# Sums of weight quarters in program order, and x_c tiles split three behind their load, in a two-layer hybrid trunk in fp32

## The chip, the cores and the metric

One core of one Trainium2 chip. The metric is the device time of the whole kernel in microseconds (us); lower is better. Three runs of the kernel before took 1402.33, 1403.09 and 1404.14 us; the median is 1403.09 us.

## What is computed

A trunk of two layers over 256 context and 256 latent tokens of width 1024, one batch element. Layer 0 mixes tokens with a bidirectional mLSTM, layer 1 with multi-head latent attention; a gated feed-forward with a convolution follows each, and every sub-layer has an adaptive shift and scale and a LayerNorm behind it. Cut to the part around the change, the inputs of the mLSTM (T is the tokens, M_INNER is 2048):

```python
def _mlstm_inputs(h, w_up, conv_w, conv_b, w_qk, w_v, w_gates, b_gates):
    x_m = h @ w_up                                        # [T, 2048]
    x_c = jax.nn.silu(_dwconv(x_m, conv_w, conv_b))       # convolution over tokens
    q, k = jnp.split(x_c @ w_qk, 2, axis=-1)
    ...
    v = (x_m @ w_v).reshape(B, T, M_HEADS, M_DV).transpose(0, 2, 1, 3)
    gates = jnp.einsum("bti,zig->zbgt", x_c, w_gates) + b_gates[:, None, :, None]
```

All of it is fp32. The kernel reaches that accuracy with three matmuls in a rounded format for each product: every operand is split into a high half (a cast) and a low half (the operand minus the cast), and high x high, high x low and low x high are added up.

## The kernel before

TensorE does one product after another: w_up, the output gate ("og"), x_m times w_v (w_v, L771 to L833), the gates (from L841), q and k, the scan, and so on. `mm3` (L373 to L377) issues the three matmuls of a product, at L375, L376 and L377.

**The stream of weights.** Weights come in "quarters" of 128 x 1024 numbers, in one fixed list. Class `Stream` (L229) takes each through three steps. `_load` (L262) issues its DMA from DRAM, from SyncE's queue (L273), into a "raw" buffer; in w_v there are several rings of such buffers. `_split` (L288) makes the halves: ScalarE casts the raw quarter to the high half (L315), then VectorE subtracts to get the low half (L318), both into one of three "w" buffers (NB = 3). `use` (L324) hands the halves to TensorE; when a quarter is done, its w buffer is free for the quarter three places on.

**The product w_v.** It is a Strassen-Winograd product: fewer matmuls, with sums of blocks of the weights in place of some blocks, and sums of partial products at the end. It has two passes, p = 0 and p = 1. Each has a first loop of 16 quarters (vt2, v11, vt3 and vt1, four times) and a second of 12 (v21, vt4 and v22, four times), and each quarter has 12 matmuls of 128 x 512. Counted along the list, pass p = 1 has the quarters 60 to 75 and 76 to 87. Of each four quarters of a first loop, three hold sums of weights that are made on the spot by `_sum` (L278): VectorE adds v12 and v22 in place (L284, the quarter vt3), adds v11 to that (L285, the quarter vt2, which has no load of its own), and adds v11 to v12 (L286, the quarter vt1). `_split` calls `_sum` four quarters ahead of the vt1 quarter (SUMS = 5 counts the quarter itself). vt2 is also written to DRAM (L317), and read back and added to v22's weights for vt4 (L270, L271).

**The tiles of x_c.** x_c was written to DRAM earlier as 16 tiles of 128 x 512 and is needed by the gates and by q and k. Pass p = 1 brings it back: `xc_load` (L696) is called between quarters, six times in the first loop and ten in the second. It takes a buffer "xcr", writes one number of the last used quarter's high half into it (`gate`, a copy of one element on ScalarE, L518: the load can then not start before that quarter was split), issues the load from ScalarE's queue (L699), casts (L380, ScalarE) and subtracts (L381, VectorE).

**Between and behind.** After each loop, VectorE adds up the partial products (L801 to L813, "the combination"; L825 to L831 after the second).

**What sets the order.** The program is written as one sequence. A scheduler puts each instruction on its engine's list; it may put one that is written later ahead of others where it reckons that it can start sooner. On the chip each engine works through its list in order, and waits at the head of the list for what the instruction needs. `tc.keep_in_program_order` takes an instruction and holds it behind the instruction that was written last before it for the same engine. It says nothing on those that are written later.

Of the kernel before, what the change touches and what calls it, by code (L numbers as in the profile page):

```python
# [228 lines left out]
class Stream:  # L229
# [48 lines left out]
    def _sum(self, j):  # L278

        key = self.order[j][0]  # L280
        if key[0] == "vt1":
            nc = self.k.nc
            t2, b11, b22, b12 = [self.raw[i] for i in range(j - 3, j + 1)]
            nc.vector.tensor_add(b22, b22, b12)  # L284
            nc.vector.tensor_add(t2, b22, b11)  # L285
            nc.vector.tensor_add(b12, b12, b11)  # L286

    def _split(self):  # L288
        k, j = self.k, self.ns
# [57 lines left out]
class K:  # L347
# [227 lines left out]
    def start_up(self):  # L575

        nc, st = self.nc, self.st
        self.hT = []
        self.xcd = self.dr.tile([16, 128, 512], F32, name="xcd")
        self.xmd = self.dr.tile([16, 128, 512], F32, name="xmd")  # L580
        self.t2d = [[self.dr.tile([128, 1024], F32, name="t2d%d%d" % (p, j)) for j in range(4)] for p in range(2)]
        self.xA, self.x1, self.xc = {}, {}, []
        w, ps, raws = [], [], []
        src = self.a["ada_w"][0]
        self.adaw, self.xT = {}, []
        for op, g in LOADS:
            f0, f1 = GROUPS[g] if op != "r" else (0, 0)
            if op == "a":
                wd = 128 * (f1 - f0)
                nk = 512 // wd  # L590
                self.adaw[g] = []
                for k in range(8):
                    if k % nk == 0:
                        t = self.uf("adaw")
                        self.adaw[g].append(t)
                    ap = bass.AP(tensor=src.tensor, offset=src.offset + k * 128 * 6 * D + f0 * 128,
                                 ap=[[6 * D, 128], [D, 2], [1, wd]])
                    c = k % nk * 2 * wd
                    nc.sync.dma_start(t[:, c:c + 2 * wd].rearrange("p (a b) -> p a b", a=2), ap)
            elif op == "x":  # L600
                for i in range(f0, f1):
                    x = self.s2("xT")
                    nc.sync.dma_start(x, self.a["tokT"][i])
                    self.xT.append(x)
            else:
                n, _ = st.ids["up", g, 0]
                r = self.pool.tile([128, 1024], F32, tag="raw" if g < 3 else "ar", name="raw0",
                                   bufs=NRAW if g < 3 else 2)
                nc.sync.dma_start(r, st.ws[n])
                raws.append(r)  # L610

        def wsplit(m):
            if m < 3:
                t = self.pool.tile([128, 2, CW], F32R, tag="w", name="w", bufs=NB)
                h, l = t[:, 0], t[:, 1]
            elif m == 3:
                h, l = [self.pool.tile([128, CW], F32R, tag="acc", name="w0", bufs=2) for _ in range(2)]
            else:
                h, l = [self.pool.tile([128, CW], F32R, tag="u", name="w0", bufs=NU) for _ in range(2)]
            self.split(h, l, raws[m])  # L620
            w.append((h, l))
            ps.append(self.ps("up"))

        def part(g, ms):
            for m in ms:
                for k in range(*GROUPS[g]):
                    c = slice(k * 128, (k + 1) * 128)
                    self.mm3(ps[m], (w[m][0][:, c], w[m][1][:, c]), (self.hT[k][:, 0], self.hT[k][:, 1]),
                             k == 0, k == 7)

        e = mybir.EngineType
        idle = self.ps("idle")
        rows = {}
        with self.tc.manual_schedule(engines={e.PE, e.DVE, e.Activation}):
            for op, g in STEPS:
                if op == "S":
                    rows[g] = self.ada_split(g)
                elif op == "A":
                    rows[g] = self.ada_rows(g, rows[g])
                elif op == "T":  # L640
                    rows[g] = self.ada_T(g, rows[g])
                elif op == "M":
                    self.ada_cols(g, rows.pop(g))
                    self.mod_tiles(range(*GROUPS[g]))
                elif op == "W":
                    wsplit(g)
                elif op == "D":
                    for _ in range(g):
                        nc.tensor.matmul(idle, self.zero[:, 0:128], self.zero, start=True, stop=True)
                else:  # L650
                    part(int(op), [g])
        for m in range(NUP):
            self.up_evac(m, ps[m])
# [40 lines left out]
            self.tick(0, ADA_U)  # L694

    def xc_load(self, k):  # L696
        x = self.s2("xcr")
        self.gate(x[0:1, 0:1])
        self.nc.scalar.dma_start(x, self.xcd[k])  # L699
        u = self.u("xc")  # L700
        self.split(u[:, 0], u[:, 1], x)
        self.xc.append(u)

    def tokmm(self, key, s, x, evac, each=None):

# [65 lines left out]
    def w_v(self):  # L771


        nc, st, A = self.nc, self.st, self.xA
        self.vd = self.dr.tile([H0, 4, 128, 512], F32, name="vd")

        def prod(ps, a, w, h, j):
            for b in range(2):
                ts = slice(b * 128, (b + 1) * 128)
                cs = slice(h * 512, (h + 1) * 512)  # L780
                self.mm3(ps[b], (a[:, 0, ts], a[:, 1, ts]), (w[0][:, cs], w[1][:, cs]), j == 0, j == 7)

        def pair(name):
            return [self.ps(name) for _ in range(2)]

        def put(s, t, v):
            nc.gpsimd.dma_start(self.vd[s, t], v)
        for p in range(2):
            p6, p1, p7, p5 = [pair("tok") for _ in range(4)]
            for i in range(4):  # L790
                for name, ps, x in (("vt2", p6, "S2"), ("v11", p1, 1), ("vt3", p7, "S3"), ("vt1", p5, "S1")):
                    w = st.use((name, p, i))
                    for h in range(2):
                        prod(ps, A[x, 2 * i + h], w, h, 2 * i + h)
                    self.tick(1)
                    if p == 1 and i and name in ("v11", "vt1"):
                        self.xc_load(len(self.xc))
            u1, u3, u4 = [], [], []
            for b in range(2):
                u = self.s2("u1")  # L800
                nc.scalar.copy(u, p1[b])  # L801
                u1.append(u)
                u = self.s2("u2")
                nc.vector.tensor_tensor(u, p6[b], u1[b], op=ALU.add)
                u4.append(u)
            for b in range(2):
                u = self.s2("u3")
                nc.vector.tensor_tensor(u, p7[b], u4[b], op=ALU.add)
                u3.append(u)
            for b in range(2):  # L810
                v = self.s2("v")
                nc.vector.tensor_tensor(v, p5[b], u3[b], op=ALU.subtract)
                nc.vector.tensor_tensor(u4[b], p5[b], u4[b], op=ALU.subtract)  # L813
                put(2 * p + 1, 2 + b, v)
            p2, p4, p3 = pair("tok"), pair("tok"), pair("tok")
            for i in range(4):
                for name, ps, x in (("v21", p2, 2), ("vt4", p4, 3), ("v22", p3, "S4")):
                    w = st.use((name, p, i))
                    for h in range(2):
                        prod(ps, A[x, 2 * i + h], w, h, 2 * i + h)  # L820
                    self.tick(1)
                    if p == 1 and len(self.xc) < 16:
                        self.xc_load(len(self.xc))
            for b in range(2):
                nc.vector.tensor_tensor(u1[b], p2[b], u1[b], op=ALU.add)  # L825
                put(2 * p, b, u1[b])
            for b in range(2):
                nc.vector.tensor_tensor(u3[b], p4[b], u3[b], op=ALU.add)
                put(2 * p, 2 + b, u3[b])
            for b in range(2):  # L830
                nc.vector.tensor_tensor(u4[b], p3[b], u4[b], op=ALU.add)  # L831
                put(2 * p + 1, b, u4[b])
        self.xA = None  # L833
# [937 lines left out]
```

## Time and profile before

The times of the profile are those of one profiled execution. Its own time and the span of its instructions are both in the table; all times within it are counted from the start of the span.

| | |
|---|---|
| median of 3 runs | 1403.09 us |
| profiled execution | 1404.94 us |
| its span | 1403.2 us |
| TensorE matmuls (PE) | 1371.7 us, 98% |
| VectorE (DVE) | 1029.9 us, 73% |
| ScalarE (ACT) | 696.0 us, 50% |
| GpSimd (POOL) | 107.4 us, 8% |
| granted TensorE clock | 0.997 |

Busy time is the sum of an engine's instructions; shares are of the span. PEld is the loading of stationary tiles, which goes on beside the matmuls. In a timeline, a row has the start, the length, the engine, the line, the operation, what it writes and reads (buffer numbers left out), the shape and how many instructions the row holds; in brackets stands how long the engine had been idle before it, and what ended that. "ACTq" and "SPq" are the issue of a DMA from ScalarE's and SyncE's queue. In a table of waits the three numbers are the idle time in all, the times, and the longest.

### The profile page before, as it was taken

The page shows a single profiled execution, that of the slowest core. Times are in us where ns is not written, and L with a number is a line of the kernel's source. Part 1 is how long each engine was busy: PE and PEld are TensorE (multiplying, and loading weights), DVE is VectorE, ACT ScalarE, POOL GpSimd, SP SyncE. Part 2 cuts the span into 40 slices and gives each one's busy share as a digit, 9 for nine tenths or more (in the row PEclk, how much of TensorE's full clock was granted, in tenths as well). Part 3 has the DMA queues.
Part 4 walks back from the last instruction along what each step waited for, and adds up shares of the span by engine and source line. Part 5 has one row for each costly group of instructions (what it writes and reads, how often), then busy time and mean ns, then how long its engine had stood idle before and what let it go on. Part 6 is the DMA issues. An engine that isn't in the chain of part 4 may idle for free.

```text
span 1403.2 us, 19109 instructions
## 1 busy us (share of the span) xinstructions
PE 1371.7 (98%) x6969; PEld 1152.3 (82%) x6969; DVE 1029.9 (73%) x1627; ACT 696.0 (50%) x1177; POOL 107.4 (8%) x193
## 2 busy tenths in 40 slices
PE   7999999998999999999999999999999999999997
PEld 3788888876788888878888888888888988999986
DVE  6597675676698596869789877754568889776773
ACT  6585444434544455365644343434364667455560
POOL 0032000011001010120001000000000001001000
PEclk9999999999999999999999999999999999999999
DMA  9588757778666463756747677765666425357750
GB/s 336 209 283 287 256 190 247 223 254 278 206 204 218 134 211 109 263 185 218 243 132 246 220 236 247 249 206 162 194 197 209 136 89 200 117 189 227 210 186 31
DMA packets 91262, 288.97 MB, mean 206 GB/s; under 512 B 11288, under 2 KB 19736, under 8 KB 91168
## 3 DMA queue, kind: packets, MB, share of 16 engines
q1 hardware_dynamic: 69824, 224.29, 48.6%
q0 software_dynamic: 15296, 50.36, 11.6%
q10 hardware_dynamic: 6048, 13.11, 2.6%
q8 instruction: 54, 0.88, 0.3%
q14 instruction: 40, 0.33, 0.1%
HBM read 261.46 MB, written 26.26 MB: 205 GB/s over the span
## 4 chain that ended last, share of the span: by engine, by line
PE 86%; DMA 6%; DVE 5%; ACT 2%; issue 1%; SPq 0%; DVEq 0%; ACTq 0%
PE fin L376 9%; PE fin L375 9%; PE fin L377 9%; PE y L376 6%; PE y L377 6%; PE y L375 5%; PE qk L375 4%; PE qk L377 4%; PE qk L376 4%; PE tok L376 4%; PE tok L377 4%; PE tok L375 4%; DMA raw<-in_ws 3%; DMA xcr<-xcd 2%; PE up L375 2%; PE up L377 2%
## 5 line engine op out<-in xcount | busy, mean ns | idle before, releaser
L318 DVE TENSOR_TENSOR w<-raw,w 128x1024 fp32r<-128x1024 f32 (+2 forms) x289 | 350.2, 1214 | 178.2 <-ACT w L315 177.8
L315 ACT CAST w<-raw 128x1024 fp32r<-128x1024 f32 (+2 forms) x289 | 301.8, 1046 | 322.5 <-PE fin L377 106.8
L376 PE MATMUL fin<-h,w 128*128 128x256 f32 (+1 forms) x696 | 231.7, 333 | 0.0
L377 PE MATMUL fin<-h,w 128*128 128x256 f32 (+1 forms) x696 | 231.4, 333 | 0.0
L375 PE MATMUL fin<-h,w 128*128 128x256 f32 (+1 forms) x696 | 231.2, 333 | 0.1
L504 DVE SCALAR_TENSOR_TENSOR junk<-ar,bc 128x1024 f32<-128x1024 f32 x128 | 155.8, 1217 | 5.5 <-ACT bc L545 3.4
L376 PEld LDWEIGHTS fin<-h,w 128*128 128x128 f32 x696 | 132.2, 190 | 12.9 <-DVE h L1196 0.2
L375 PEld LDWEIGHTS fin<-h,w 128*128 128x128 f32 x696 | 131.9, 190 | 13.2 <-ACT h L1195 0.3
L377 PEld LDWEIGHTS fin<-h,w 128*128 128x128 f32 x696 | 132.2, 190 | 12.7
L375 PE MATMUL qk<-xc,w 128*128 128x512 f32 x256 | 100.7, 393 | 0.0
L377 PE MATMUL qk<-xc,w 128*128 128x512 f32 x256 | 99.9, 390 | 0.0
L376 PE MATMUL qk<-xc,w 128*128 128x512 f32 x256 | 99.8, 390 | 0.0
L375 PE MATMUL y<-w,act 128*128 128x512 f32 (+1 forms) x212 | 80.4, 379 | 0.0
L376 PE MATMUL y<-w,act 128*128 128x512 f32 (+1 forms) x212 | 80.1, 378 | 0.0
L377 PE MATMUL y<-w,act 128*128 128x512 f32 (+1 forms) x212 | 80.1, 378 | 0.0
L375 PEld LDWEIGHTS qk<-xc,w 128*128 128x128 f32 x256 | 48.1, 188 | 10.1 <-issue 0.4
L377 PEld LDWEIGHTS qk<-xc,w 128*128 128x128 f32 x256 | 48.1, 188 | 9.9
L376 PEld LDWEIGHTS qk<-xc,w 128*128 128x128 f32 x256 | 48.1, 188 | 9.7
L318 DVE TENSOR_TENSOR wu<-raw,wu 128x1024 fp32r<-128x1024 f32 x36 | 43.5, 1220 | 13.0 <-ACT wu L315 12.4
L375 PE MATMUL up<-hT,w 128*128 128x512 f32 x128 | 50.5, 394 | 0.5 <-ACT hT L380 0.5
L665 ACT ACTIVATE fg<-fg 128x512 f32<-128x512 f32 (+1 forms) x44 | 23.0, 523 | 56.0 <-DVE fg L663 52.8
L376 PE MATMUL up<-hT,w 128*128 128x512 f32 x128 | 50.1, 392 | 0.4 <-DVE hT L381 0.4
(397 smaller groups left out, 2930.6 us busy)
## 6 DMA issues: line engine op xcount, KB each, us to landing
raw<-in_ws SPq DMA_DIRECT2D x306, 512.0 KB, 4.3
ar<-in_adaT SPq DMA_DIRECT2D x80, 512.0 KB, 4.5
adaw<-in_ada_w SPq DMA_DIRECT2D x32, 256.0 KB, 5.9
xmd<-xr POOLq DMA_DIRECT2D x16, 256.0 KB, 4.8
xcd<-cv POOLq DMA_DIRECT2D x16, 256.0 KB, 4.6
xs<-xmd POOLq DMA_DIRECT2D x16, 256.0 KB, 6.5
od<-o ACTq DMA_DIRECT2D x16, 256.0 KB, 3.0
t2d<-raw ACTq DMA_DIRECT2D x8, 512.0 KB
```

The lines of the kernel that those rows point to most:

```text
L315: k.nc.scalar.copy(h[:, :cols], src)
L318: k.nc.vector.tensor_sub(l[:, :cols], src, h[:, :cols])
L375: mm(out, w[0], x[0], start=start, stop=False)
L376: mm(out, w[0], x[1], start=False, stop=False)
L377: mm(out, w[1], x[0], start=False, stop=stop)
L504: nc.vector.scalar_tensor_tensor(o, w, 1.0, self.bc[j], op0=ALU.mult, op1=ALU.mult, accum_out=col[:, k, j:j + 1])
L665: nc.scalar.activation(tmp[:, :n], tmp[:, :n], AF.Silu)
```

## The change

Two things. The three additions of `_sum` are held to program order on VectorE. And `xc_load` is taken apart: the load is issued as before, but without the one-element copy ahead of it and held to program order on ScalarE; the cast and the subtraction of a tile come three calls later, the cast held to program order as well. The waiting tiles stand in a list `xcr`. To have three calls more, the first loop calls it in its first round too, at vt1 (seven calls), and the second loop calls it until all 16 tiles are split (twelve calls, the last three without a load).

```diff
         if key[0] == "vt1":
-            nc = self.k.nc
+            nc, pin = self.k.nc, self.k.tc.keep_in_program_order
             t2, b11, b22, b12 = [self.raw[i] for i in range(j - 3, j + 1)]
-            nc.vector.tensor_add(b22, b22, b12)
-            nc.vector.tensor_add(t2, b22, b11)
-            nc.vector.tensor_add(b12, b12, b11)
+            pin(nc.vector.tensor_add(b22, b22, b12))
+            pin(nc.vector.tensor_add(t2, b22, b11))
+            pin(nc.vector.tensor_add(b12, b12, b11))
...
     def xc_load(self, k):
-        x = self.s2("xcr")
-        self.gate(x[0:1, 0:1])
-        self.nc.scalar.dma_start(x, self.xcd[k])
-        u = self.u("xc")
-        self.split(u[:, 0], u[:, 1], x)
-        self.xc.append(u)
+
+        pin = self.tc.keep_in_program_order
+        if k < 16:
+            x = self.s2("xcr")
+            pin(self.nc.scalar.dma_start(x, self.xcd[k]))
+            self.xcr.append(x)
+        if len(self.xcr) > 3 or k >= 16:
+            x = self.xcr.pop(0)
+            u = self.u("xc")
+            pin(self.nc.scalar.copy(u[:, 0], x))
+            self.nc.vector.tensor_sub(u[:, 1], x, u[:, 0])
+            self.xc.append(u)
...
-                    if p == 1 and i and name in ("v11", "vt1"):
-                        self.xc_load(len(self.xc))
+                    if p == 1 and (name == "vt1" or i and name == "v11"):
+                        self.xc_load(len(self.xc) + len(self.xcr))
...
                     if p == 1 and len(self.xc) < 16:
-                        self.xc_load(len(self.xc))
+                        self.xc_load(len(self.xc) + len(self.xcr))
```

In the changed kernel the load stands in L701, the cast in L706, the subtraction in L707, and the combination six lines further down (L804 becomes L810, L813 becomes L819, L831 becomes L837). TensorE's order is as before. The order on VectorE and ScalarE differs between the output gate and the gates, and nowhere else.

VectorE at the start of pass p = 1, before. The subtractions (L318) read the raw quarters 61 (raw_2159), 62 (raw_2176), 63 (raw_2193) and 64 (raw_2210, a vt2); raw_2226, raw_2243 and raw_2260 are the quarters 65 to 67, raw_2277, raw_2293, raw_2313 and raw_2331 the quarters 68 to 71.

```order
L318 TENSOR_TENSOR w_2345<-raw_2159,w_2345 128x1024
L831 TENSOR_TENSOR u2_2132<-tok_2154,u2_2132 128x512
L831 TENSOR_TENSOR u2_2136<-tok_2155,u2_2136 128x512
L284 TENSOR_TENSOR raw_2313<-raw_2313,raw_2331 128x1024
L318 TENSOR_TENSOR w_2381<-raw_2176,w_2381 128x1024
L285 TENSOR_TENSOR raw_2277<-raw_2313,raw_2293 128x1024
L285 TENSOR_TENSOR raw_2210<-raw_2243,raw_2226 128x1024
L318 TENSOR_TENSOR w_2401<-raw_2193,w_2401 128x1024
L286 TENSOR_TENSOR raw_2331<-raw_2331,raw_2293 128x1024
L318 TENSOR_TENSOR w_2418<-raw_2210,w_2418 128x1024
```

The same place in the changed kernel:

```order
L318 TENSOR_TENSOR w_2381<-raw_2176,w_2381 128x1024
L284 TENSOR_TENSOR raw_2243<-raw_2243,raw_2260 128x1024
L318 TENSOR_TENSOR w_2401<-raw_2193,w_2401 128x1024
L285 TENSOR_TENSOR raw_2210<-raw_2243,raw_2226 128x1024
L286 TENSOR_TENSOR raw_2260<-raw_2260,raw_2226 128x1024
L318 TENSOR_TENSOR w_2418<-raw_2210,w_2418 128x1024
L318 TENSOR_TENSOR w_2436<-raw_2226,w_2436 128x1024
L318 TENSOR_TENSOR w_2455<-raw_2243,w_2455 128x1024
L284 TENSOR_TENSOR raw_2313<-raw_2313,raw_2331 128x1024
L285 TENSOR_TENSOR raw_2277<-raw_2313,raw_2293 128x1024
L286 TENSOR_TENSOR raw_2331<-raw_2331,raw_2293 128x1024
L318 TENSOR_TENSOR w_2476<-raw_2260,w_2476 128x1024
```

The sums of the quarters 68 to 71 moved from ahead of the subtraction of quarter 62 to behind that of quarter 66, and now stand three in a row. So do those of six other groups in the two passes, one of them with a small subtraction in between.

ScalarE in the first loop of pass p = 1, before. The casts L315 are of the quarters 68, 69, 70 and 71; xcr and xc are the raw and the split tiles of x_c.

```order
L315 CAST w_2497<-raw_2277 128x1024
L380 CAST xc_2536<-xcr_2533 128x512
L315 CAST w_2515<-raw_2293 128x1024
L518 COPY xcr_2576<-w_2515 1x1
L699 DMA xcr_2576<-xcd_97 128x512
L317 DMA t2d13_106<-raw_2348 128x1024
L315 CAST w_2539<-raw_2313 128x1024
L380 CAST xc_2579<-xcr_2576 128x512
L315 CAST w_2559<-raw_2331 128x1024
```

The changed kernel, the casts of the quarters 70 to 74:

```order
L701 DMA xcr_2531<-xcd_97 128x512
L315 CAST w_2533<-raw_2313 128x1024
L315 CAST w_2553<-raw_2331 128x1024
L701 DMA xcr_2570<-xcd_97 128x512
L706 CAST xc_2572<-xcr_2453 128x512
L317 DMA t2d13_106<-raw_2348 128x1024
L315 CAST w_2575<-raw_2348 128x1024
L315 CAST w_2594<-raw_2384 128x1024
L701 DMA xcr_2611<-xcd_97 128x512
L706 CAST xc_2613<-xcr_2493 128x512
L315 CAST w_2616<-raw_2404 128x1024
```

Before, a tile's cast stands one weight cast behind its load. After, the cast that follows a load is that of the tile loaded three calls earlier.

VectorE at the combination after the first loop, before; raw_2439, raw_2456 and raw_2477 are the quarters 76, 77 and 78.

```order
L318 TENSOR_TENSOR w_2665<-raw_2439,w_2665 128x1024
L381 TENSOR_TENSOR xc_2700<-xcr_2697,xc_2700 128x512
L804 TENSOR_TENSOR u2_2709<-tok_2374,u1_2707 128x512
L808 TENSOR_TENSOR u3_2711<-tok_2377,u2_2705 128x512
L318 TENSOR_TENSOR w_2682<-raw_2456,w_2682 128x1024
L808 TENSOR_TENSOR u3_2713<-tok_2378,u2_2709 128x512
L812 TENSOR_TENSOR v_2715<-tok_2379,u3_2711 128x512
L813 TENSOR_TENSOR u2_2705<-tok_2379,u2_2705 128x512
L812 TENSOR_TENSOR v_2719<-tok_2380,u3_2713 128x512
L813 TENSOR_TENSOR u2_2709<-tok_2380,u2_2709 128x512
L318 TENSOR_TENSOR w_2729<-raw_2477,w_2729 128x1024
```

The changed kernel; raw_2458, raw_2479 and raw_2499 are the quarters 77, 78 and 79.

```order
L318 TENSOR_TENSOR w_2673<-raw_2458,w_2673 128x1024
L707 TENSOR_TENSOR xc_2690<-xcr_2570,xc_2690 128x512
L810 TENSOR_TENSOR u2_2695<-tok_2373,u1_2693 128x512
L318 TENSOR_TENSOR w_2719<-raw_2479,w_2719 128x1024
L810 TENSOR_TENSOR u2_2699<-tok_2374,u1_2697 128x512
L814 TENSOR_TENSOR u3_2701<-tok_2377,u2_2695 128x512
L814 TENSOR_TENSOR u3_2703<-tok_2378,u2_2699 128x512
L818 TENSOR_TENSOR v_2705<-tok_2379,u3_2701 128x512
L819 TENSOR_TENSOR u2_2695<-tok_2379,u2_2695 128x512
L818 TENSOR_TENSOR v_2709<-tok_2380,u3_2703 128x512
L819 TENSOR_TENSOR u2_2699<-tok_2380,u2_2699 128x512
L318 TENSOR_TENSOR w_2739<-raw_2499,w_2739 128x1024
```

The subtraction of quarter 78 moved ahead of the combination, which now stands ahead of that of quarter 79.

More of the change, by code (lines that the diff above doesn't have):

```diff
@@ L581, in start_up @@
         self.t2d = [[self.dr.tile([128, 1024], F32, name="t2d%d%d" % (p, j)) for j in range(4)] for p in range(2)]
-        self.xA, self.x1, self.xc = {}, {}, []
+        self.xA, self.x1, self.xc, self.xcr = {}, {}, [], []
         w, ps, raws = [], [], []
```

## Prediction

> **What bounds the kernel now.** I read the page's busy shares first, then a table of windows by stage, then TensorE's timeline where that table shows idle time, and then the waits and the timelines of the two engines that feed it.
>
> ```profile
> span 1403.2 us, 19109 instructions
> PE 1371.7 (98%) x6969; PEld 1152.3 (82%) x6969; DVE 1029.9 (73%) x1627; ACT 696.0 (50%) x1177; POOL 107.4 (8%) x193
> ...
> core 0: us, PE busy (x) PEld busy (x) DVE busy (x) ACT busy (x) POOL busy (x), PEclk, DMA share, GB/s
> 165.00:267.00 102.00, 102.00 (x451) 84.49 (x450) 63.55 (x76) 42.15 (x54) 5.23 (x7) 1.00 0.73 234
> 267.00:372.00 105.00, 97.56 (x421) 78.11 (x420) 76.44 (x87) 47.92 (x71) 10.07 (x16) 1.00 0.73 231
> 372.00:600.00 228.00, 227.97 (x1057) 186.11 (x1055) 176.15 (x335) 107.74 (x217) 22.83 (x43) 1.00 0.58 195
> ```
>
> TensorE is the bound: 98% of the span at a granted clock of 1.00. So an edit on VectorE or ScalarE can only give back time in which TensorE waits. Pass p=0 of the weight product (all of 165 to 267 us) has none. The window from 267 to 372 us, which holds pass p=1, has 105 − 97.56 = 7.44 us. The change has work in both passes, and nothing of it after 372 us. TensorE's timeline shows where the 7.44 us lie (the last number in brackets is idle time and what ended it):
>
> ```profile
> 285.86 0.39 PE L375 MATMUL tok<-w,s 128*128 128x512 f32 x1
> ...
> 291.30 0.39 PE L375 MATMUL tok<-w,s 128*128 128x512 f32 x1
> 294.24 0.50 PE L376 MATMUL tok<-w,s 128*128 128x512 f32 x1 [2.55 <-DVE w L318]
> 294.57 0.40 PE L377 MATMUL tok<-w,s 128*128 128x512 f32 x1
> ...
> 296.88 0.39 PE L375 MATMUL tok<-w,x 128*128 128x512 f32 x1
> 297.64 0.50 PE L376 MATMUL tok<-w,x 128*128 128x512 f32 x1 [0.37 <-DVE w L318]
> 297.98 0.40 PE L377 MATMUL tok<-w,x 128*128 128x512 f32 x1
> ...
> 320.47 0.50 PE L376 MATMUL tok<-w,x 128*128 128x512 f32 x1 [0.76 <-DVE w L318]
> ...
> 332.87 0.49 PE L375 MATMUL tok<-w,x 128*128 128x512 f32 x1 [1.26 <-ACT w L315]
> 334.13 0.50 PE L376 MATMUL tok<-w,x 128*128 128x512 f32 x1 [0.77 <-DVE w L318]
> ...
> 343.56 0.50 PE L376 MATMUL tok<-w,s 128*128 128x512 f32 x1 [0.98 <-DVE w L318]
> ...
> 355.65 0.50 PE L376 MATMUL tok<-w,xm 128*128 128x512 f32 x1 [0.76 <-DVE w L318]
> ...
> 371.88 2.00 PE L841 MATMUL gates<-xc,w 128*32 128x512 f32 x8
> ```
>
> Pass p=1 begins at 285.86 us (quarter 60) and ends where the gates begin, at 371.88: 86.02 us. It has 28 quarters of 12 matmuls, 336. Undisturbed, the 24 matmuls from 285.86 to 291.30 take 5.44 us, 0.2267 us each and 2.72 us a quarter. 336 × 0.2267 = 76.2 us. **The pass loses 86.0 − 76.2 = 9.85 us.** That is more than the 7.44 us of idle time, since the matmul that restarts after a wait is slower (0.50 in place of 0.39 us, counted as busy). All seven waits are for the two halves of a weight quarter, ScalarE's cast (L315) or VectorE's subtraction (L318).
>
> The two waits at 294 and 297 us together: (294.57 − 291.30) + (297.98 − 296.88) less four pitches is 4.37 − 0.91 = 3.46 us. The other five: 9.85 − 3.46 = 6.4 us. These two groups have different causes.
>
> **The change part by part.** *The sums.* ScalarE's casts, then VectorE's rows, around the first two waits:
>
> ```profile
> 286.06 1.06 ACT L315 CAST w<-raw 128x1024 fp32r<-128x1024 f32 x1 [1.66 <-PE tok L377]
> 288.78 1.05 ACT L315 CAST w<-raw 128x1024 fp32r<-128x1024 f32 x1 [1.66 <-PE tok L377]
> ...
> 291.82 1.23 DVE L284 TENSOR_TENSOR raw<-raw 128x1024 f32<-128x1024 f32 x1 [3.71 <-DMA raw<-in_ws]
> 292.96 1.22 DVE L318 TENSOR_TENSOR w<-raw,w 128x1024 fp32r<-128x1024 f32 x1
> 294.10 2.35 DVE L285 TENSOR_TENSOR raw<-raw 128x1024 f32<-128x1024 f32 x2
> 296.37 1.22 DVE L318 TENSOR_TENSOR w<-raw,w 128x1024 fp32r<-128x1024 f32 x1
> ```
>
> Quarter 62 was cast by 287.12 us, but its L318 stood behind a sum (L284) of quarters 68 to 71, whose load landed only at 291.82. TensorE wanted the low half at 291.53. Quarter 63 was cast by 289.83, and its L318 then stood behind two more sums. In the new order the L318 of quarter 62 comes first, then the L284 of quarters 64 to 67, and the sums of 68 to 71 wait until the L318 of quarter 66. These sums cannot wait for that late load. Both waits go: −3.46 us.
>
> What the pins add: elsewhere three sums now stand in a row between the L318 of two neighbouring quarters, 3 × 1.14 = 3.4 us (1.14 is the step from 292.96 to 294.10). No sum is added, only their place. Is there room? The ring has three buffers, so the cast of quarter i starts when quarter i−3 is done (the 1.66 us waits above), and i's low half is needed two quarters and one matmul later: 5.44 + 0.23 = 5.67 us. L318 of i−1 ends 1.05 + 1.22 = 2.3 us after its own buffer came free, which is 2.72 us earlier than i's. So L318 of i ends 2.3 + 3.4 + 1.2 − 2.72 = 4.2 us after its buffer came free, with some 1.4 us to spare. Cost: 0, as long as the four quarters have landed when their sums come up. With them 1.4 us late it begins to show. No row of before has three sums in a row; the nearest (294.10, two in a row) ended in a wait of 0.37 us, so I bound this at 0 to 0.37 us for each of the seven groups placed so, 0 to 2.6 in all, and take 0, since the 0.37 had the late sum ahead of it.
>
> *The x_c tiles.* Their rows, the wait they cause, and two of its consequences:
>
> ```profile
> L699 ACTq DMA_DIRECT2D xcr<-xcd x16: 326/326/327, 298.8 to 362.2; - x16
> L380 ACT CAST xc<-xcr x16: 610/620/622, 302.9 to 365.6; 128x512 fp32r<-128x512 f32 x16
> DMA to landing us min/median/max: 4.1/5.9/7.6
> ...
> ACT xc L380 <- DMA xcr<-xcd: 24.7, 12, 5.2
> ...
> 317.58 0.62 ACT L380 CAST xc<-xcr 128x512 fp32r<-128x512 f32 x1 [5.18 <-DMA xcr<-xcd]
> 318.11 1.05 ACT L315 CAST w<-raw 128x1024 fp32r<-128x1024 f32 x1
> ...
> 331.25 0.62 ACT L380 CAST xc<-xcr 128x512 fp32r<-128x512 f32 x1 [4.76 <-DMA xcr<-xcd]
> 331.78 1.04 ACT L315 CAST w<-raw 128x1024 fp32r<-128x1024 f32 x1
> ...
> 319.19 1.23 DVE L318 TENSOR_TENSOR w<-raw,w 128x1024 fp32r<-128x1024 f32 x1 [0.26 <-ACT w L315]
> ```
>
> ScalarE waits in order for a tile it loaded a moment ago, 12 times, 24.7 us. Behind that wait stands the cast of a quarter TensorE is about to need: 317.58, then 318.11, then L318 at 319.19, then the matmul at 320.47; and 331.25, 331.78, then the matmul at 332.87. Now the cast comes three tiles later. In the first loop tiles are two quarters apart, so that is 3 × 5.44 = 16.3 us after the issue, in the second 3 × 2.72 = 8.2 us, against a slowest landing of 7.6. The wait goes, and with it −6.4 us. The margin is thin only in the second loop, 0.6 us at the slowest landing, 2.3 at the median. A miss by up to the quarter's own slack, 5.67 − 2.3 = 3.4 us, is still hidden.
>
> The Trainium skill ("DMA: Bandwidth & Descriptors", section "Issuing engines are not separate DMA queues") speaks against this: transfers started from different engines run on the same 16 engines and interleave, so four x_c loads in flight would stretch one another and the weight loads. No run here shows four at once yet; by that rule the 6.4 us would be wholly or partly given back (rival A).
>
> *What is late next.* The fifth wait (343.56) is also due to the combination of the first partial products, which stood ahead of its L318:
>
> ```profile
> 339.31 0.68 DVE L808 TENSOR_TENSOR u<-tok,u 128x512 f32<-128x512 f32 x1
> ...
> 342.30 2.35 DVE L318 TENSOR_TENSOR w<-raw,w 128x1024 fp32r<-128x1024 f32 x2
> ```
>
> Five operations, 339.31 to 342.30, 3.0 us. In the new order seven of them, 7 × 0.6 = 4.2 us, stand one quarter later, ahead of the L318 of quarter 79. By the same reckoning that L318 ends 0.65 us before it is needed. I take 0; the bounds are 0 and the 0.98 us of that row. The gates need the last x_c tile, which is now cast three steps later, one quarter before they start; they use it last, so 0, at most its cast and subtraction (1 us).
>
> *The rest.* The 16 gate copies leave ScalarE, which is not the bound: 0.
>
> ```profile
> L518 ACT COPY xcr<-w x16: 180/186/191, 298.6 to 362.0; 1x1 f32<-1x1 f32 x16
> ```
>
> The loads are now held by program order alone. After the gates the order on all engines is as before, so the gain is carried to the end: from 372 to 600 us TensorE waits 0.03 us.
>
> **Sum.** −3.46 − 6.4 = −9.85 at most; 0.35 us I keep for the small costs above, so −9.5. The profiled execution took 1404.94 us (its span 1403.2): 1395.4. The median of the runs, 1403.09, is 1.85 us below it: **1393.6 us**.
>
> **The rivals.** *A, the x_c loads get in each other's way.* The stretch in which they run is nearly full:
>
> ```profile
> 300.00:337.00 37.00, 34.22 (x148) 27.19 (x148) 22.37 (x23) 17.48 (x25) 2.65 (x3) 1.00 0.89 276
> ```
>
> With a DMA share of 0.89, landings of 7.6 us could pass 8.2 us, or weight quarters come late in their place. Then only the sums' part is gained: 1403.09 − 3.46 = 1399.6 us. Against it: the amount moved is the same, each load only starts earlier, and 16.3 us is ample where the share is highest. 0.14.
>
> *B, nothing is gained.* The waits could come from the ring of three buffers, to which ScalarE's casts are tied anyway; whatever is hurried then waits for a buffer: 1403.1 us. The Trainium skill ("Perfetto Trace Analysis", section "Optimization Strategy") says that a gap that repeats on the engine that should be saturated can mean too few buffers. Against it: from 165 to 267 us the same ring feeds TensorE without any wait. 0.08.
>
> *C, slower: the three pinned sums hold back the L318 behind them.* A late sum can cost much, as the first of all shows:
>
> ```profile
> 173.21 1.23 DVE L284 TENSOR_TENSOR raw<-raw 128x1024 f32<-128x1024 f32 x1 [6.78 <-DMA raw<-in_ws]
> ```
>
> If each of the eight groups met its loads 3.71 us late, as the row at 291.82, 2.3 us would be left after the slack of 1.4: 8 × 2.3 − 9.85 = +8.6, 1411.7 us. It turns to slower where the groups wait over 1.4 + 9.85/8 = 2.6 us on average. For it: the pins take from VectorE the freedom to run the next L318 first. Against it: in this trace the sums were early, not their loads late; they come later now, and the 6.78 us above cost TensorE nothing. 0.06.
>
> **How the numbers follow.** Forecast 0.72: 1403.09 − 9.85 = 1393.2 with nothing in the way, down to 1392.0 by the spread of the runs (1402.33 to 1404.14, about 1 us to a side), up to 1396.8 by the bounds of 2.6 and 0.98 us. A 0.14, B 0.08, C 0.06. The range reaches up to A's time, 1392.0 to 1399.7 us, and leaves out some 0.17. A measurement can tell 0.2% (2.8 us). Faster by more: forecast and most of A, 0.84. Within: B and the rest of A, 0.10. Slower: 0.06.
>
> **What would show it.** After the change, TensorE's idle time in pass p=1 under 1 us and the pass 76 to 77 us long; no L284 waiting for a load ahead of an L318 that is ready; ScalarE's waits for x_c loads near 0. Rival A shows as L706 waiting for its load with TensorE waiting behind it, B as casts that wait for TensorE while TensorE waits for them, C as TensorE waiting for the L318 that follows L286. A pass still over 84 us makes the forecast wrong.

## The result, and the profile after

Over four runs the changed kernel took 1393.97 us (median; 1393.14 to 1394.95), beside it the kernel before 1402.71 us (1400.79 to 1404.14). The ratio is 0.9939, 95% interval 0.9922 to 0.9956: 8.6 us less (10.9 to 6.2). The forecast was 1393.6 us, a fall of 9.5. The profiled execution took 1394.95 us, 9.99 less than that of before. One run of the kernel "block of 4" below was a slow one of 6273.72 us, and its median, ratio and interval are those of the other, fast runs.

The page and the table of windows of the changed kernel, cut at the same stages as before:

```profile
span 1393.2 us, 19087 instructions
PE 1368.5 (98%) x6969; PEld 1152.3 (83%) x6969; DVE 1030.5 (74%) x1627; ACT 694.2 (50%) x1161; POOL 107.6 (8%) x193
...
165.00:267.00 102.00, 102.00 (x451) 84.46 (x450) 63.84 (x73) 42.17 (x52) 5.23 (x7) 1.00 0.70 225
267.00:362.00 95.00, 95.00 (x419) 77.82 (x418) 76.06 (x88) 45.89 (x56) 10.09 (x16) 1.00 0.80 263
300.00:337.00 37.00, 37.00 (x164) 30.32 (x163) 28.79 (x33) 18.86 (x23) 4.66 (x6) 1.00 0.97 298
362.00:590.00 228.00, 227.97 (x1060) 186.59 (x1058) 175.42 (x334) 106.65 (x216) 23.55 (x44) 1.00 0.56 190
```

The idle 7.44 us of the second window are gone: TensorE is busy in all of its 95 us. Its timeline gives the ends of pass p = 1:

```profile
284.26 0.39 PE L375 MATMUL tok<-w,s 128*128 128x512 f32 x1
...
360.70 0.62 PE L847 MATMUL gates<-xc,w 128*32 128x512 f32 x2
```

The pass takes 360.70 − 284.26 = 76.44 us in place of 86.02: 9.58 us less. The rest of the difference between the two executions is not the change's: the pass begins 1.6 us earlier (285.86 against 284.26), which arose in the first 17 us, where the order of instructions is the same; and from the gates to the end of the span it took 1032.5 in place of 1031.3 us, most of it one wait that the trace of before does not have:

```profile
1057.85 0.44 PE L1369 MATMUL ckT<-ident,ckr 128*128 128x128 f32 x2 [0.82 <-DVE ckr L1321]
```

9.58 + 1.6 − 1.2 = 9.98.

VectorE at the start of the pass, the place of the early sum:

```profile
286.42 1.22 DVE L318 TENSOR_TENSOR w<-raw,w 128x1024 fp32r<-128x1024 f32 x1
287.55 1.22 DVE L284 TENSOR_TENSOR raw<-raw 128x1024 f32<-128x1024 f32 x1
288.69 1.22 DVE L318 TENSOR_TENSOR w<-raw,w 128x1024 fp32r<-128x1024 f32 x1
289.82 1.22 DVE L285 TENSOR_TENSOR raw<-raw 128x1024 f32<-128x1024 f32 x1
290.96 1.22 DVE L286 TENSOR_TENSOR raw<-raw 128x1024 f32<-128x1024 f32 x1
292.24 1.23 DVE L318 TENSOR_TENSOR w<-raw,w 128x1024 fp32r<-128x1024 f32 x1
```

No sum waits here (no brackets), nor does one wait for a load anywhere in the two passes, and quarter 62 is subtracted at 286.42, more than 3 us before TensorE begins it at 289.70. ScalarE in the first loop, with the issue, the late cast and the next weight cast, then its waits for x_c in all:

```profile
314.43 1.05 ACT L315 CAST w<-raw 128x1024 fp32r<-128x1024 f32 x1 [1.66 <-PE tok L377]
314.45 0.33 ACTq L701 DMA_DIRECT2D xcr<-xcd  x1
315.39 0.61 ACT L706 CAST xc<-xcr 128x512 fp32r<-128x512 f32 x1
...
ACT xc L706 <- DMA xcr<-xcd: 0.4, 1, 0.4
```

24.7 us in 12 waits have become 0.4 us in one. ScalarE now waits for TensorE to free a buffer (the 1.66 us above), which is the side on which one wants the wait.

### The profile page after: what moved, and what is told of

Same layout as the page of the kernel before. It is cut to its first block, busy times and chain, and to the rows that moved or that the text cites. A ratio compares the mean times of both kernels' runs of the same rounds, so it can differ in the third digit from the quotient of the medians.

```text
span 1393.2 us, 19087 instructions
## 1 busy us (share of the span) xinstructions
PE 1368.5 (98%) x6969; PEld 1152.3 (83%) x6969; DVE 1030.5 (74%) x1627; ACT 694.2 (50%) x1161; POOL 107.6 (8%) x193
## 4 chain that ended last, share of the span: by engine, by line
PE 91%; DVE 3%; ACT 2%; DMA 2%; issue 1%; SPq 0%; DVEq 0%; ACTq 0%
PE fin L375 9%; PE fin L376 9%; PE fin L377 9%; PE tok L375 6%; PE tok L377 6%; PE tok L376 6%; PE y L376 5%; PE y L377 5%; PE y L375 5%; PE qk L375 4%; PE qk L377 4%; PE qk L376 4%; PE up L375 2%; PE up L377 2%; PE up L376 2%; DMA raw<-in_ws 2%
## 5 line engine op out<-in xcount | busy, mean ns | idle before, releaser
L318 DVE TENSOR_TENSOR w<-raw,w 128x1024 fp32r<-128x1024 f32 (+2 forms) x289 | 350.7, 1215 | 202.8 <-ACT w L315 202.1
L315 ACT CAST w<-raw 128x1024 fp32r<-128x1024 f32 (+2 forms) x289 | 302.2, 1046 | 345.2 <-PE fin L377 107.0
L318 DVE TENSOR_TENSOR wu<-raw,wu 128x1024 fp32r<-128x1024 f32 x36 | 43.5, 1221 | 13.4 <-ACT wu L315 13.1
```

The lines of the kernel that those rows point to most:

```text
L315: k.nc.scalar.copy(h[:, :cols], src)
L318: k.nc.vector.tensor_sub(l[:, :cols], src, h[:, :cols])
```

## The experiments

Twelve kernels, in three groups that each shared a chip and the runs of the kernel before (medians 1403.38, 1403.28 and 1403.82 us), five rounds each. A ratio is to those, and need not be the quotient of the two medians; what a kernel gained in us is taken from the ratio. "Lost" is read from the trace of each: the time between the starts of neighbouring matmuls beyond the pitch of 0.2267 us, for all gaps over 0.27 us between 60 us and the gates. It is 9.6 us before and 0.25 us after.

| kernel | median us | ratio | 95% interval | lost us |
|---|---|---|---|---|
| only the sums | 1399.36 | 0.9975 | 0.9962 to 0.9987 | 4.7 |
| only x_c | 1395.60 | 0.9948 | 0.9929 to 0.9967 | 2.5 |
| x_c none behind | 1399.76 | 0.9973 | 0.9962 to 0.9985 | 6.6 |
| x_c one behind | 1396.77 | 0.9957 | 0.9944 to 0.9969 | 3.3 |
| x_c two behind | 1393.41 | 0.9934 | 0.9920 to 0.9948 | 0.25 |
| copies kept | 1394.20 | 0.9938 | 0.9924 to 0.9952 | 0.6 |
| x_c not in program order | 1393.23 | 0.9927 | 0.9913 to 0.9941 | 0 |
| the same, none behind | 1394.19 | 0.9940 | 0.9925 to 0.9955 | 0.6 |
| block of 3 (control) | 1394.33 | 0.9937 | 0.9924 to 0.9950 | 1.0 |
| block of 4 | 1397.25 | 0.9951 | 0.9936 to 0.9966 | 3.5 |
| block of 5 | 1402.70 | 0.9993 | 0.9984 to 1.0002 | 8.4 |
| block of 6 | 1412.48 | 1.0061 | 1.0046 to 1.0076 | 18.4 |

### Each half by itself

The sums alone: the kernel before with the three additions held to program order.

```diff
-            nc.vector.tensor_add(b22, b22, b12)
+            pin(nc.vector.tensor_add(b22, b22, b12))
...
```

> Only the sums are held to program order; x_c is loaded, cast and subtracted as before. Theory (two separate causes, each an instruction that waits for a load ahead of one that is ready): the two waits at the start of pass p=1 go (-3.5 us), the x_c waits stay (6.4 us lost), so the pass takes 82.5 us and the kernel 1399.2 us; ScalarE's x_c casts still wait some 25 us for their loads. Rival 1 (the x_c part is the whole cause): 1402.7 us. Rival 2 (the sums are the whole cause): 1394 us.

1399.36 us, 3.5 us less than before by the ratio (5.3 to 1.8). TensorE's waits in the trace of this run:

```profile
326.26 0.50 PE L375 MATMUL tok<-w,x 128*128 128x512 f32 x1 [0.62 <-ACT w L315]
327.52 0.50 PE L376 MATMUL tok<-w,x 128*128 128x512 f32 x1 [0.76 <-DVE w L318]
...
337.22 0.50 PE L376 MATMUL tok<-w,s 128*128 128x512 f32 x1 [1.11 <-DVE w L318]
...
349.40 0.50 PE L376 MATMUL tok<-w,xm 128*128 128x512 f32 x1 [0.76 <-DVE w L318]
...
ACT xc L380 <- DMA xcr<-xcd: 19.9, 11, 4.4
```

The two at the start are gone; those behind x_c loads stay, one fewer, and ScalarE waits 19.9 us for x_c in place of the expected 25. Both rivals fall.

x_c alone: the changed kernel with the sums as they were.

```diff
-            pin(nc.vector.tensor_add(b22, b22, b12))
+            nc.vector.tensor_add(b22, b22, b12)
...
```

> Only the x_c part of the change; the sums are free as before, and the sum of the quarters 68 to 71 stands ahead of the subtraction of quarter 62 again. Theory: the x_c waits go (-6.4 us), the early sum costs its 3.5 us as before, so the pass takes 79.7 us and the kernel 1396.3 to 1397.5 us, with the wait of about 2.5 us at the second matmul of quarter 62 back. Rival 1 (the x_c part is the whole cause): 1394 us. Rival 2 (the sums are the whole cause): 1402.7 us.

1395.60 us, 7.3 us less (10.0 to 4.6), and 0.7 us below the expected range. The early sum is back on VectorE, and TensorE waits behind it:

```profile
288.88 1.23 DVE L284 TENSOR_TENSOR raw<-raw 128x1024 f32<-128x1024 f32 x1 [2.32 <-DMA raw<-in_ws]
290.02 1.22 DVE L318 TENSOR_TENSOR w<-raw,w 128x1024 fp32r<-128x1024 f32 x1
...
291.30 0.50 PE L376 MATMUL tok<-w,s 128*128 128x512 f32 x1 [1.19 <-DVE w L318]
...
294.70 0.50 PE L376 MATMUL tok<-w,x 128*128 128x512 f32 x1 [0.38 <-DVE w L318]
```

It is the same place with a smaller wait (1.19 in place of 2.55 us): the sum waited 2.32 us for its load in place of 3.71. What such a sum costs is thus set by when one transfer happens to land. The two halves give 3.5 and 7.3 us, and the whole 8.6: they add up within their intervals. By the lost time of the traces they are 4.9 and 7.1 us, more than the 9.4 of the whole, for each half alone also made waits of the other shorter (19.9 in place of 24.7 us for x_c, 2.32 in place of 3.71 for the sum).

### How far behind, and what else was changed with it

Distance 0, with all else of the change:

```diff
-        if len(self.xcr) > 3 or k >= 16:
+        if len(self.xcr) > 0 or k >= 16:
```

> The changed kernel with distance 0: each x_c tile is cast and subtracted in the call that loads it; the copies are left out and the order is held as in the change. Theory (the distance is what counts): ScalarE waits for landings again, 3 us or more each and over 10 in all, and most of the 6.4 us is back: 1398 to 1403 us. Rival (the one-element copies that held back the loads were the cause): 1394 us, and no wait of ScalarE for x_c.

1399.76 us. ScalarE waits again:

```profile
ACT xc L706 <- DMA xcr<-xcd: 24.9, 10, 5.4
...
324.71 0.62 ACT L706 CAST xc<-xcr 128x512 fp32r<-128x512 f32 x1 [4.11 <-DMA xcr<-xcd]
...
331.09 0.62 ACT L706 CAST xc<-xcr 128x512 fp32r<-128x512 f32 x1 [3.85 <-DMA xcr<-xcd]
```

It is nearly the 24.7 us of before, so in program order the distance is what removes the wait. Of the 6.6 us lost in this trace, 1.6 are no wait: behind the longest wait of TensorE (2.22 us, ended at 333.19) eight matmuls follow each other at 0.43 in place of 0.23 us, in a stretch of 3.4 us of lower clock (granted 0.57 from 333 to 337 us). The wait of 2.55 us in the trace of before had no such stretch behind it, so what brings it stays open.

Distance 1 (`> 1` in the same line):

> The changed kernel with distance 1. Theory: in the first loop one tile is 5.4 us, more than the landing of 4.4 us; in the second it is 2.7 us, so that ScalarE waits there some 1.7 us a tile, and since the next load is issued behind that cast, two tiles take 4.4 + 0.6 + 1.1 + 0.3 = 6.4 us where TensorE takes 5.4. Nine tiles lose 4 us, of which a quarter's slack of 3.4 us hides most: 1394 to 1396 us. Rival (the landing is a matter of how many loads are in flight, so fewer is faster): no wait, 1394 us; rival (any wait of ScalarE is paid in full): 1398 us or more.

1396.77 us: 6.0 us less than before (7.9 to 4.4), so some 3 us of the gain are missing; the trace has 3.3 us lost. The expectation of at most 2 was too low. The second loop waits as reckoned, but a wait at the combination had not been counted:

```profile
328.15 0.62 ACT L706 CAST xc<-xcr 128x512 fp32r<-128x512 f32 x1 [1.56 <-DMA xcr<-xcd]
328.67 0.58 ACT L807 COPY u<-tok 128x512 f32<-128x512 f32 x1
...
329.31 0.50 PE L375 MATMUL tok<-w,xm 128*128 128x512 f32 x1 [1.09 <-ACT u L807]
...
339.64 0.62 ACT L706 CAST xc<-xcr 128x512 fp32r<-128x512 f32 x1 [3.48 <-DMA xcr<-xcd]
...
344.62 0.50 PE L376 MATMUL tok<-w,s 128*128 128x512 f32 x1 [0.76 <-DVE w L318]
```

Behind the wait of ScalarE at 328.15 stands not only a weight cast but the copy (L807) that frees an accumulator, for which TensorE waits 1.09 us.

Distance 2 (`> 2`):

> The changed kernel with distance 2. Theory: two tiles are 5.4 us in the second loop, more than the usual landing of 4.4 us, and three tiles must take 6.4 us where TensorE takes 8.2: 0 to 0.5 us lost, 1394 to 1394.5 us. Rival (each tile of distance is worth the same, so half of what distance 1 lost): 1395.5 us.

1393.41 us, 0.25 us lost, as with three. ScalarE waits 1.3 us for x_c, in two waits, and TensorE waits behind neither. Two is enough.

The copies put back, with distance 3:

```diff
             x = self.s2("xcr")
+            pin(self.nc.scalar.copy(x[0:1, 0:1], self.st.last[0:1, 0:1].bitcast(F32)))
             pin(self.nc.scalar.dma_start(x, self.xcd[k]))
```

> The changed kernel with the 16 one-element copies put back on ScalarE, each ahead of its load and held to program order too. Theory (the copies cost nothing where ScalarE waits anyway): 1394 us. Rival (the copies were part of the gain): 16 x 0.19 = 3 us, 1397 us.

1394.20 us: the copies cost nothing that shows.

Load and cast of x_c freed from program order, without copies, distance 3:

```diff
-            pin(self.nc.scalar.dma_start(x, self.xcd[k]))
+            self.nc.scalar.dma_start(x, self.xcd[k])
...
-            pin(self.nc.scalar.copy(u[:, 0], x))
+            self.nc.scalar.copy(u[:, 0], x)
```

> The changed kernel with x_c three tiles behind, but load and cast of x_c not held to program order: the scheduler then puts the first seven loads far ahead and gathers the casts in clumps of up to four, and in the second loop a cast stands one or two quarters behind its load. Theory (what counts is how long a load has had before ScalarE meets its cast): no waits in the first loop, waits of 1 to 3 us in the second, 1 to 4 us lost, 1395 to 1398 us. Rival (written distance alone does it, program order is not needed): 1394 us. Rival (without program order all is lost again): 1400 us.

1393.23 us and nothing lost. The expectation was wrong: program order for x_c is not needed for the gain. From its trace, issue to cast is 56.3 to 60.5 us for the first seven tiles, which the scheduler moved ahead into pass p = 0, and 4.2 to 10.2 us for the other nine. ScalarE waits 2.8 us in four waits, and each is inside a quarter's slack. Its interval overlaps that of the changed kernel, so it isn't shown to be faster.

The same with distance 0:

> The kernel of the run before (x_c neither held to program order nor preceded by a copy), with distance 0 in place of 3. The scheduler puts the first seven loads far ahead by itself; in the second loop a cast stands at most one quarter behind its load. Theory (how long a load has had, however it comes about): the first loop loses nothing, the second loses 3 to 4.5 us, 1397 to 1398.5 us. Rival 1 (written distance is what counts): as with distance 0 in program order, 1399.8 us. Rival 2 (leaving out the copies is what counts): 1393.2 us.

1394.19 us; wrong again, and more tellingly. This kernel loads, casts and subtracts in the same call, as the kernel before did, and loses 0.6 us in its trace in place of 9.6. From the kernel with only the sums (ratio 0.9975 against 0.9940, intervals apart) it differs by two things: it makes one call of `xc_load` more in the first loop, and it lacks the copy that had tied each load to a recent quarter. Without it the scheduler issues the first seven loads 32 to 57 us ahead of their casts. In the second loop ScalarE still meets loads that have not landed, and it costs little:

```profile
339.24 0.62 ACT L706 CAST xc<-xcr 128x512 fp32r<-128x512 f32 x1 [4.74 <-DMA xcr<-xcd]
339.26 0.33 ACTq L701 DMA_DIRECT2D xcr<-xcd  x1
339.76 1.05 ACT L315 CAST w<-raw 128x1024 fp32r<-128x1024 f32 x1
...
342.13 0.49 PE L376 MATMUL tok<-w,s 128*128 128x512 f32 x1 [0.33 <-DVE w L318]
```

Beside the 4.76 us wait of before (331.25), after which TensorE waited 1.26 and 0.77 us, this one of 4.74 us costs 0.33 and the slower restart: it began 6.9 us before TensorE wanted the quarter behind it (at 341.41), that of before 5.0 us (at 331.45). The expectation took each wait at its length; what counts is how much of it lies beyond the slack. The time from issue to cast, tile by tile, read from the timelines of ScalarE:

```
before               4.1  3.1  7.7  3.8  6.2  2.6  3.1  6.4  6.6  6.0  6.6  2.8  4.4  3.5  3.5  3.4
changed             17.2 17.3 17.2 17.3 17.5 12.6  9.4  6.9  8.8  9.1  9.1  8.4  9.1  9.1  8.5  9.1
free, none behind   32.3 39.1 39.1 55.0 57.2 55.9 55.4  3.7  3.8  8.4  7.6  4.1  2.9  2.6  3.3  2.7
```

The first row agrees with the prediction's slowest landing of 7.6 us, which rests on few loads: the trace of before tells the landing of two of the 16 alone (4.1 and 7.6 us), but where ScalarE waits for its tile, issue to cast is the landing, and that is at most 7.7.

So the copies were a cause after all, in the program in which the scheduler is free: they made the loads late. There are two ways to the same end: issue early, or cast later. The change took away the copies and did the second; with the second the copies don't matter (1394.20 us), and without them and without program order the second isn't needed (1394.19 us).

### What the row of sums costs

Further operations of a sum's size behind the three, and the subtractions of w_v's quarters held to program order, so that the whole block stands ahead of the next one.

```diff
             pin(nc.vector.tensor_add(b12, b12, b11))
+            pin(nc.vector.tensor_tensor(b12, b12, b12, op=ALU.max))
...
-            k.nc.vector.tensor_sub(l[:, :cols], src, h[:, :cols])
+            d = k.nc.vector.tensor_sub(l[:, :cols], src, h[:, :cols])
+            if key[0][0] == "v":
+                k.tc.keep_in_program_order(d)
```

The control, without a further operation:

> The control for the three longer blocks: no operation added, only the subtractions of w_v's quarters held to program order. If the blocks cost what is over their slack, 1394 to 1395.5 us, with the two waits of 0.6 to 1.1 us at the combinations that the block of four also showed, since these now stand ahead of a subtraction. If it is 1397.5 us as with the block of four, the added operation cost nothing at all.

One more:

> The changed kernel with one more VectorE operation of a sum's size behind each three sums (the maximum of the vt1 quarter with itself, which changes nothing), and the subtractions of w_v's quarters held to program order, so that a block of four stands in a row. Theory (a block costs what is over its slack): L318 of the quarter before ends 2.4 us after its buffer came free, four operations take 4.56, the next L318 1.22, together 8.2 us against 2.72 + 5.67 = 8.4: nothing to 1 us lost, 1394 to 1395 us. Rival C (the block is on the path of TensorE from the start): 8 x 1.14 = 9 us, 1403 us.

Two more:

> The same with two more operations. Theory: 0.9 us late in each of the groups, some six to eight of them, and 2 us in the one that has two operations of the combination in between: 6 to 9 us, 1400 to 1403 us; TensorE then waits for the L318 behind the block. Rival C: 18 us, 1412 us. Rival (VectorE is never on the path, it is the loads alone): 1394 us.

Three more:

> The same with three more operations. Theory: 2.1 us late in each group and about 4 us in the one with the combination in between: 14 to 19 us, 1408 to 1413 us. From block to block the cost is 1.14 us a group once the slack is used up. Rival C: 27 us, 1421 us. Rival (VectorE is never on the path): 1394 us.

1394.33, 1397.25, 1402.70 and 1412.48 us: steps of 2.9, 5.5 and 9.8 us, and by the lost time of the traces 2.5, 4.9 and 10.0. The control shows that there is slack at three. The times of the blocks of five and six are as expected; the block of four cost 2.3 us more than expected at the most. TensorE's waits for VectorE's subtraction in the blocks of three, four, five and six (in the last two also its waits for ScalarE's cast, which no expectation had), then a block of four in full:

```profile
PE tok L378 <- DVE w L318: 0.4, 1, 0.4
...
PE tok L379 <- DVE w L319: 1.3, 2, 0.9
...
PE tok L380 <- DVE w L320: 2.9, 5, 1.2
PE tok L379 <- ACT w L317: 1.7, 6, 0.3
...
PE tok L381 <- DVE w L321: 10.8, 7, 2.2
PE tok L380 <- ACT w L318: 2.0, 7, 0.3
...
232.45 1.22 DVE L284 TENSOR_TENSOR raw<-raw 128x1024 f32<-128x1024 f32 x1
233.71 1.22 DVE L285 TENSOR_TENSOR raw<-raw 128x1024 f32<-128x1024 f32 x1
234.85 1.22 DVE L286 TENSOR_TENSOR raw<-raw 128x1024 f32<-128x1024 f32 x1
236.10 1.22 DVE L287 TENSOR_TENSOR raw<-raw 128x1024 f32<-128x1024 f32 x1
237.25 3.49 DVE L319 TENSOR_TENSOR w<-raw,w 128x1024 fp32r<-128x1024 f32 x3
...
238.52 0.50 PE L379 MATMUL tok<-w,x 128*128 128x512 f32 x1
238.86 0.40 PE L380 MATMUL tok<-w,x 128*128 128x512 f32 x1
```

The four take 4.80 us, 1.20 each, since a sum that reads what the one ahead has just written starts 1.25 us behind it and not 1.14. The subtraction then ends at 238.4, and the second matmul of the quarter begins about 0.1 us late (0.33 us behind the first in place of 0.23). So a block of three has some 1.1 us to spare, and not the 1.4 reckoned. Five blocks are late by as little; the other part of the step is one wait of 0.92 us, in the group that has operations of the combination next to it, where there was less room from the start.

The eight groups do not pay alike. In the block of six TensorE loses 2.3 to 3.0 us at each of six groups, 0.6 at the last and nothing at the first. Two groups lose 1.24 us each in the block of five and 2.5 in that of six: the step of a further operation (1.25), now that no slack is left. And 1.5 us of the block of six are a stretch at the lower clock (0.57 from 294 to 298 us), as with distance 0, so that its step of 9.8 us is not that of the operations alone.

## Why the prediction was right, point by point

**The loss of 9.85 us in the pass.** Right: 9.58 us of it went in the profiled executions, with the forecast at 9.5. The runs say 8.6 (10.9 to 6.2), so that the match to 0.1 us is closer than the runs can tell.

**The sums, −3.46 us.** Right in place and cause; alone they gave 3.5 us (5.3 to 1.8). That the wait was one late transfer ahead of a ready subtraction is shown by the kernel with only x_c changed, in which the sum's wait for its load fell from 3.71 to 2.32 us and TensorE's by as much, from 2.55 to 1.19. That the size came out so near is in part luck, since the same sum costs 2.1 in place of 3.5 us there.

**The block of three, 0 us.** Right: no wait stands behind a block in the changed kernel. The slack was 1.1 us in place of 1.4; 0.1 of that is the step between dependent sums, taken at 1.14 us, and the rest is open.

**x_c, −6.4 us.** Right in size (7.3, interval 10.0 to 4.6, alone). But the prediction treated the distance as the cause of the gain and the loss of the copies as worth 0. With the program order that the change brings, both statements hold (1399.76 us at distance 0; 1394.20 us with the copies back). The step that was incomplete is the reason why the loads of before were issued so late. It had gone by ScalarE's timeline, where the load stands a quarter ahead of its cast, and hadn't asked what put it there: the copy. So leaving out the copies, "0" in the prediction, is worth about as much as the distance where the scheduler may move the loads: 4.9 us between the kernel with only the sums and the one that is free and at distance 0, the one call more included.

**The margins.** The second loop's 8.2 us against a slowest landing of 7.6 was called thin. For ScalarE it was: one tile waited 0.44 us, cast 6.9 us behind its issue, since two loads had been issued together there. For TensorE it is not: at a distance of two, 5.4 us there, ScalarE waits 1.3 us in all and TensorE loses nothing more, so a quarter's slack absorbs the waits, as the prediction had said of small misses.

**What is late next.** (The wait at 343.56 is the sixth of the seven, not the fifth.) 0.35 us was kept for small costs, and the changed kernel has 0.25, at another place. TensorE's weight load waits not for the subtraction of quarter 79, but for an accumulator that the combination frees:

```profile
PEld tok L375 <- DVE u L810: 0.4, 1, 0.4
```

Quarter 79 is subtracted in time behind its seven operations. Where subtractions are held to program order (the control), the combination stands ahead of quarter 78, whose subtraction is then late: TensorE waits 0.4 us for it. The gates met no x_c tile that was late.

**Rival A, loads that get in each other's way.** Its price is not there, and its mechanism is not shown. The rows of DMA issues for weight quarters, from the start of the pass to the gates (KB each, median us from issue to landing), before and after, then the landings of the x_c loads after:

```profile
raw<-in_ws SPq DMA_DIRECT2D x13, 512.0 KB, 6.6
...
raw<-in_ws SPq DMA_DIRECT2D x14, 512.0 KB, 8.8
...
DMA to landing us min/median/max: 2.8/4.4/4.5
```

Each of the two medians is of one load alone, since the traces tell no landing of the others, so that 6.6 and 8.8 us show no trend. The DMA share from 300 to 337 us rose from 0.89 to 0.97, in a stretch that holds 164 matmuls in place of 148, and TensorE waits for no quarter. The x_c loads are hardly in flight together: in the first loop one is issued every 5.4 us, and the two landings on record there took 4.5 and 4.4. At the start of the second loop four are, for a moment (issued at 331.0, 331.4, 333.7 and 336.4; the first, by ScalarE's wait, landed at 337.9, after 6.9 us), and that is no longer than the slowest of before. The Trainium skill ("DMA: Bandwidth & Descriptors", section "Issuing engines are not separate DMA queues") says that transfers interleave whichever engine started them; no run here shows it either way.

**Rival B, the ring of three buffers.** Falls: the same ring now feeds TensorE for 76 us with 0.25 us lost. ScalarE's waits for TensorE are the ring at work and cost nothing.

**Rival C, the row of sums.** Its condition, sums that wait for their loads, did not come about: no sum waits for one in the changed kernel. That a row which ends too late holds up the L318 behind it, and what that costs, is shown by the blocks. Three operations more put the kernel 8.6 us above the kernel before (ratio 1.0061). The pins are safe here by a little less than one operation (1.1 us of slack, 1.25 for an operation).

What stays open: the 0.82 us wait at 1057.85 and the 1.6 us of the start-up weren't tried; both lie where the two programs have the same order.

## What to carry to other kernels

An engine works through its list in order, so ask of every instruction that waits for a transfer what stands behind it and when that is needed; the wait costs what exceeds that slack, not its length. Give such an instruction time by issuing its load earlier or by consuming it later, and look first for what holds the load back: here a copy of one element did. When a list is held to program order, count the block that then stands in a row against the slack: one operation too many in each group gave back 2 to 3 us, three gave back twice the gain.

## What had not been expected of the hardware

Two VectorE additions of 128 x 1024 in fp32 follow each other at 1.14 us when they are independent and at 1.25 us when the second reads what the first wrote (233.71 − 232.45 = 1.26, 234.85 − 233.71 = 1.14, 236.10 − 234.85 = 1.25). A matmul that restarts after a wait takes some 0.50 in place of 0.39 us in the rows shown here, even where the wait was 0.1 us (238.52), and delays the next by 0.1, so the five blocks that were 0.1 us late cost 0.2 us each. And in two of the traces a wait of TensorE (2.22 us with distance 0, 2.2 in the block of six) was followed by some 3 us in which matmuls came at 0.43 us (granted clock 0.57), where the 2.55 us of before were not.
